# Weight parts exactly 2048 bytes apart, moving operands placed 64 bytes lower modulo 512, and a bias table of 16 copies

## The chip, the cores and the metric

The kernel runs on one core of one Trainium2 chip. The metric is the device time of one execution in microseconds, as the median of several runs.

## What is computed

Two layers of a decoder trunk on 256 tokens of width 2048, in float32. Layer 0 mixes with compressed, selected and sliding-window attention (8 heads) beside a retention group; layer 1 mixes with a gated delta rule (32 heads). Each layer then has cross-attention into 256 memory tokens and a SwiGLU FFN of hidden width 5632. Cut to its frame:

```python
def reference(x, mem, rel_bias, ...):
    h = x
    for layer in range(DEPTH):
        hn = rms_norm(h, ln_mix[layer])
        if layer % 2 == 0:
            mix = nsa_retention_mixer(hn, hyb_w_in[e], hyb_w_out[e], ..., rel_bias)
        else:
            mix = gated_deltanet_mixer(hn, gdn_w_in[o], ..., gdn_w_out[o])
        h = h + mix
        h = h + memory_cross_attention(rms_norm(h, ln_mem[layer]), mem, ...)
        h = h + swiglu_ffn(rms_norm(h, ln_ffn[layer]), ffn_w_in[layer], ffn_w_out[layer])
    return h
```

Inside the attention a bias per head depends on the distance of query and key alone: `rel_bias[rel_bucket(dist)]`.

## The kernel before

Nearly all work is projections, and all weights are read from HBM once. A projection (`Proj`, L228 by way of `passes`) takes blocks of 512 weight columns. SyncE loads 512 KB at a time (`load_weight`, L212: two rows of 128 inputs by 512 columns) into `wp`, four buffers. ScalarE rounds each row to float32r as `w_hi` (L205), VectorE forms the remainder `w_lo` (L206), both into the pool `wh`, four buffers of each. The activations are split likewise into a high and a low part (`x_hi`, `x_lo`; `hh`, `hl` in the FFN; `moh`, `mol` and others). TensorE then forms three products of each row: high by high, low by high, high by low.

In most projections the weights stand in the array (128 x 128) and the activations move, 256 columns a matmul, 12 matmuls for a weight row of 512 columns. Where the result is wanted by tokens (kind "t" in `Proj.row`), the activations stand and the weights move, 512 columns a matmul, six for a row. Moving data and the next matmul's weights both come from SBUF.

Where a tile lies in SBUF follows from its pool: pools and the tiles in them stand one behind the other in the order in which they are opened and asked for. `wh` gives every buffer the size of the largest tile asked of it. That is the row of 536 columns (2144 bytes) of the one projection in `nsa_keys` that has 256 + 280 columns, so its buffers stand 2144 bytes apart, and the pools behind it follow from there.

The bias table: `rel_bias_tiles` forms, for 8 heads, a row `f` of 400 biases by distance, on 8 partitions. It writes this row 128 times for each head to the HBM tensor `d_bias` (L735), and reads it back (L738) with a step of 399, so that each of 128 partitions of `tbias` gets its row shifted by one. Both DMAs are issued by POOL. The next ones on POOL's queue are `d_v` and `d_k` of the cross-attention (L541, L540), written when their tiles are done.

Small tasks (heads, norms, the solver) are generators that `tick` advances between the projection's matmuls; the final order on each engine is the scheduler's, from its own estimate. `invert` runs a triangular inverse on VectorE beside projections of layer 1.

Of the kernel before, what the change touches and what calls it, by code (L numbers as in the profile page):

```python
# [10 lines left out]
F32 = mybir.dt.float32  # L11
F32R = mybir.dt.float32r
# [6 lines left out]
P = 128  # L19
# [59 lines left out]
def trunk(ctx: ExitStack, tc: tile.TileContext, a: dict, out: bass.AP, phases=ALL):  # L79
    nc = tc.nc  # L80
    V, S, G, PE = nc.vector, nc.scalar, nc.gpsimd, nc.tensor
# [3 lines left out]
    wp = ctx.enter_context(tc.tile_pool(name="wp", bufs=4))  # L85
    wh = ctx.enter_context(tc.tile_pool(name="wh", bufs=4))
    sp = ctx.enter_context(tc.tile_pool(name="sp", bufs=2))
    dp = ctx.enter_context(tc.tile_pool(name="dp", bufs=1, space=DRAM))
    psj = ctx.enter_context(tc.tile_pool(name="psj", bufs=4, space=PSUM))
    psg = ctx.enter_context(tc.tile_pool(name="psg", bufs=4, space=PSUM))  # L90

    def pool(name, bufs=1, side=None):
        return tc.tile_pool(name=name, bufs=bufs, side=side, reuse_waits="tile")
# [3 lines left out]


    tasks = []
    state = {"now": 0, "banks": 4}  # L100

    class Task:
        def __init__(self, gen):
# [25 lines left out]
    def take(n):  # L129

        while state["banks"] < n:
            yield 1
        state["banks"] -= n

    def give(n):
        state["banks"] += n

    def bank(name="g"):
        return psg.tile([P, 512], F32, tag="g", name=name)
# [55 lines left out]


    def split_weight(w, g=None):
        h = wh.tile(list(w.shape), F32R, tag="wh", name="w_hi")
        l = wh.tile(list(w.shape), F32R, tag="wl", name="w_lo")
        if g is not None:  # L200

            state["hi"] = S.activation(h, w, AF.Copy, scale=g)
            V.scalar_tensor_tensor(l, w, g, h.bitcast(F32), ALU.mult, ALU.subtract)
            return h, l
        state["hi"] = S.activation(h, w, AF.Copy)  # L205
        V.tensor_sub(l, w, h.bitcast(F32))  # L206
        return h, l
# [81 lines left out]
    def proj(W, c0, segs, x, KT=KD, g=None):  # L289
        return Proj(W, c0, segs, x, KT, g).run()  # L290
# [39 lines left out]
    def split_x(tp):  # L330
        xh = tp.tile([P, KD, T], F32R, name="x_hi")
        xl = tp.tile([P, KD, T], F32R, name="x_lo")
        return xh, xl

    def fill_x(x, which, layer, rb=None):
        for k in range(KD):
            fill_k(x, which, layer, k, rb)
        return parts(x)
# [206 lines left out]
    def cross_attention(l, side):  # L545
        with pool("xax", side=side) as xx, pool("xas") as xs, pool("xa", 2) as xp:
            xb = split_x(xx)
            x = fill_x(xb, 1, l)
            kt = xs.tile([P, 4, T], F32, name="kt")
            vt = xs.tile([P, 2, 512], F32, name="vt")  # L550
            S.dma_start(kt, kv[l][0])
            S.dma_start(vt, kv[l][1])
            ec = xs.tile([P, 2], F32, name="ec")
            oh = xs.tile([P, 4, T], F32R, name="xoh")
            ol = xs.tile([P, 4, T], F32R, name="xol")

            def stat():

                yield from take(1)
                token_stat(ec)  # L560
                give(1)
                V.tensor_scalar(ec, ec, EPS, EPS * EPS, ALU.mult, ALU.add)

            def head(h, src):
                q = xp.tile([P, T], F32, tag="q", name="q")
                S.activation(q, src, AF.Copy)
                yield 1
                yield from take(2)
                sc, b2 = bank("sc"), bank("qT")
                st = xp.tile([P, 12], F32, tag="st", name="st")  # L570
                token_sumsq(q, [st[:, 6:7], st[:, 7:8]], b2)
                for t in range(2):
                    PE.matmul(sc[:, t * 256 : (t + 1) * 256], q[:, t * P : (t + 1) * P], kt[:, h, :], start=True, stop=True)
                V.scalar_tensor_tensor(st[:, 6:8], st[:, 6:8], 1.0 / P, ec, ALU.mult, ALU.add)
                rq = st[:, 8:10]
                rsqrt_(rq, st[:, 6:8], st[:, 10:12])
                s3 = sc.rearrange("p (t m) -> p t m", t=2)
                V.tensor_reduce(st[:, 0:2], s3, AX.X, ALU.max)
                V.scalar_tensor_tensor(st[:, 0:2], st[:, 0:2], -1.0, rq, ALU.mult, ALU.mult)
                p = xp.tile([P, 2, 256], F32, tag="p", name="p")  # L580
                for t in range(2):
                    S.activation(
                        p[:, t, :], s3[:, t, :], AF.Exp, scale=rq[:, t : t + 1], bias=st[:, t : t + 1],
                        accum_out=st[:, 2 + t : 3 + t],
                    )
                V.reciprocal(st[:, 4:6], st[:, 2:4])
                for t in range(2):
                    V.tensor_scalar_mul(p[:, t, :], p[:, t, :], st[:, 4 + t : 5 + t])
                yield 4
                for t in range(2):  # L590
                    for m in range(2):
                        PE.transpose(sc[:, m * 256 + t * P : m * 256 + (t + 1) * P], p[:, t, m * P : (m + 1) * P], ident)
                pT = xp.tile([P, 512], F32, tag="pT", name="pT")
                S.activation(pT, sc, AF.Copy)
                yield 1
                o = b2[:, 256:512]
                for m in range(2):
                    PE.matmul(o, vt[:, m, h * P : (h + 1) * P], pT[:, m * 256 : (m + 1) * 256], start=m == 0, stop=m == 1)
                S.activation(oh[:, h], o, AF.Copy)
                V.tensor_sub(ol[:, h], o, oh.bitcast(F32)[:, h])  # L600
                give(2)

            hs = []
            for h in range(4):
                pq = proj(a["xa_wq"][l], h * P, [("f", P)], x)[0]
                if h == 0:
                    finish([spawn(stat())])
                hs.append(spawn(head(h, pq[0][:, 0, :])))

            def xo(k):  # L610
                finish(hs[k : k + 1])
                return oh[:, k, :], ol[:, k, :]

            residual(a["xa_wo"][l], xo, 4, early=3, free=True)
# [75 lines left out]
    def mix0(xb, close):  # L690
        W = a["hyb_w_in"][0]
        done = {}
        with pool("m0o") as op:
            oh = op.tile([P, 16, T], F32R, name="moh")
            ol = op.tile([P, 16, T], F32R, name="mol")
            cm = op.tile([P, 512 + 4 * 384 + 1], F32, name="cmix")
            S.dma_start(cm, a["c_mix"])
            with pool("ns") as np_:
                x = parts(xb)
                ck = pool("cmpk", side="right")  # L700
                nsa, cmp = nsa_keys(W, x, np_, ck.__enter__(), cm)
                with pool("nt", 2) as nt:
                    for blk in range(2):
                        pq = proj(W, blk * 512, [("f", 512)], x)[0]
                        for i in range(4):
                            h = blk * 4 + i
                            q = nt.tile([P, T], F32, tag="q", name="q", bufs=8)
                            S.activation(q, pq[i // 2][:, i % 2, :], AF.Copy)
                            done[h] = spawn(nsa(nt, h, q, oh, ol))
                    finish(cmp)  # L710
                    ck.__exit__(None, None, None)
                    with pool("rt", 2) as rt_:
                        retention(W, x, rt_, oh, ol, cm, done)

                        def mo(k):
                            finish([done[k]])
                            return oh[:, k, :], ol[:, k, :]

                        residual(a["hyb_w_out"][0], mo, 16, early=12)
                        drain()  # L720
            close()

    def rel_bias_tiles(tp, rp):

        rbt = rp.tile([33, 8], F32, name="rbt")
        G.memset(rbt[32:33, :], 1.0)
        S.dma_start(rbt[:32, :], a["rel_bias"])
        ohs = rp.tile([33, 400], F32, name="ohs")
        S.dma_start(ohs, a["c_onehot"])
        b = bank()  # L730
        PE.matmul(b[:8, :400], rbt, ohs, start=True, stop=True)
        f = rp.tile([8, 400], F32, name="frev")
        V.tensor_copy(f, b[:8, :400])
        d = dp.tile([8, P, 400], F32, name="d_bias")
        G.dma_start(d, f[:, None, :].to_broadcast([8, P, 400]))  # L735
        tb = tp.tile([P, 8, 272], F32, name="tbias")

        G.dma_start(tb, bass.AP(d.tensor, d.offset + 127, [[399, P], [P * 400, 8], [1, 272]]))  # L738
        return tb

    def nsa_keys(W, x, np_, ck, cm):
# [774 lines left out]
```

## Time and profile before

| | |
|---|---|
| median of 3 runs | 3120.89 us (3120.4 to 3122.44) |
| the profiled execution | 3124.7 us, of it the span 3122.9 us |
| TensorE busy | 3042.0 us, 22,981 matmuls |
| VectorE busy | 2040.2 us |
| ScalarE busy | 1702.7 us |
| read from HBM | 549 MB, 181 GB/s over the span with what is written |

Matmuls are pipelined: the duration of one reaches beyond the start of the next. How fast TensorE goes is therefore read from starts, either of neighbouring rows in the timeline or as the length of a stretch over the number of matmuls in it. The trace leaves buffer numbers out of names; which buffer a weight row uses follows from the built program's order.

### The profile page before, as it was taken

How to read it: one execution, taken by the hardware profiler on the slowest of the kernel's cores; microseconds unless marked ns; L12 is line 12 of the kernel's file. 1: busy time of each engine (PE TensorE's matmuls, PEld its weight loads, DVE VectorE, ACT ScalarE, POOL GpSimd, SP SyncE). 2: the span in 40 equal slices, each digit the busy share in tenths (PEclk: the TensorE clock that was granted, in tenths of full speed). 3: DMA queues.
4: the chain of work that ended last, by engine and by line, in shares of the span. 5: the costliest groups of instructions: out<-in, count | busy, mean ns of one | idle time of the engine just before them, and what ended most of it. 6: DMA issues, size and time to landing. Idle time of an engine off the chain costs nothing.

```text
span 3122.9 us, 59624 instructions
## 1 busy us (share of the span) xinstructions
PE 3042.0 (97%) x22981; PEld 2912.5 (93%) x22981; DVE 2040.2 (65%) x3879; ACT 1702.7 (55%) x3316; POOL 108.8 (3%) x146
## 2 busy tenths in 40 slices
PE   9799999999999999999989978999999999999999
PEld 8699899999999999999978978999999999999887
DVE  6576776776555555557679967887567555565554
ACT  6456555664444454446655646776556444445444
POOL 0000000000000000000110100222000000000000
PEclk9899999999999999999999989999999999999999
DMA  7576545656666665556687557654555666666554
GB/s 236 145 237 197 156 130 178 189 167 187 185 184 188 184 188 184 188 186 181 178 226 220 173 151 200 175 156 126 187 182 176 184 183 187 184 186 183 196 197 164
DMA packets 340026, 569.99 MB, mean 183 GB/s; under 512 B 43844, under 2 KB 83828, under 8 KB 339612
## 3 DMA queue, kind: packets, MB, share of 16 engines
q1 hardware_dynamic: 333376, 550.79, 59.1%
q0 software_dynamic: 3056, 9.26, 1.2%
q10 hardware_dynamic: 3308, 6.14, 0.6%
q8 instruction: 180, 2.95, 0.4%
q14 instruction: 106, 0.87, 0.1%
HBM read 549.16 MB, written 15.37 MB: 181 GB/s over the span
## 4 chain that ended last, share of the span: by engine, by line
PE 94%; DMA 2%; DVE 2%; SPq 1%; ACT 0%; issue 0%; POOL 0%; DVEq 0%; ACTq 0%; POOLq 0%
PE pj L228 87%; DMA w<-in_hyb_w_in 1%; SPq L1344 1%; PE cmp L228 1%; DMA w<-in_gdn_w_in 1%; PE slv L1426 0%; PE slv L1437 0%; DVE w_lo L206 0%; PE slv L1440 0%; DVE xT L415 0%; DMA d_T<-AB 0%; DVE x_lo L348 0%; DMA mraw<-in_mem 0%; PE slv L1434 0%; PE slv L1420 0%
## 5 line engine op out<-in xcount | busy, mean ns | idle before, releaser
L206 DVE TENSOR_TENSOR w_lo<-w,w_hi 128x512 fp32r<-128x512 f32 x1938 | 1334.0, 693 | 951.2 <-ACT w_hi L205 937.8
L205 ACT ACTIVATE w_hi<-w 128x512 fp32r<-128x512 f32 x1938 | 1220.8, 632 | 1238.9 <-PE pj L228 968.3
L228 PE MATMUL pj<-x_hi,w_hi 128*128 128x256 f32 (+1 forms) x4496 | 1264.3, 283 | 50.4 <-ACT w_hi L205 50.1
L228 PE MATMUL pj<-x_lo,w_hi 128*128 128x256 f32 x4496 | 1265.6, 284 | 0.0
L228 PE MATMUL pj<-x_hi,w_lo 128*128 128x256 f32 (+1 forms) x4496 | 1241.8, 283 | 0.3 <-DVE w_lo L206 0.2
L228 PEld LDWEIGHTS pj<-x_hi,w_hi 128*128 128x128 f32 (+1 forms) x4496 | 848.9, 189 | 52.4 <-ACT w_hi L205 50.7
L228 PEld LDWEIGHTS pj<-x_lo,w_hi 128*128 128x128 f32 x4496 | 850.0, 189 | 1.1 <-issue 0.2
L228 PEld LDWEIGHTS pj<-x_hi,w_lo 128*128 128x128 f32 (+1 forms) x4496 | 836.0, 189 | 2.0 <-DVE w_lo L206 1.1
L228 PE MATMUL pj<-hh,w_hi 128*128 128x256 f32 x704 | 197.1, 281 | 0.0
L228 PE MATMUL pj<-hl,w_hi 128*128 128x256 f32 x704 | 197.1, 281 | 0.0
L228 PE MATMUL pj<-o,w_hi 128*128 128x256 f32 x1024 | 192.8, 287 | 3.0 <-ACT o L996 1.8
L228 PE MATMUL pj<-hh,w_lo 128*128 128x256 f32 x704 | 195.5, 280 | 0.0
L228 PE MATMUL pj<-w_lo,x_hi 128*128 128x512 f32 (+2 forms) x448 | 173.7, 388 | 3.4 <-DVE w_lo L206 3.4
L228 PE MATMUL pj<-w_hi,x_lo 128*128 128x512 f32 (+2 forms) x448 | 171.5, 383 | 0.0
L228 PEld LDWEIGHTS pj<-o,w_hi 128*128 128x128 f32 x1024 | 160.9, 192 | 4.1 <-ACT o L996 2.3
L228 PE MATMUL pj<-w_hi,x_hi 128*128 128x512 f32 (+2 forms) x448 | 145.6, 387 | 4.6 <-ACT w_hi L205 4.6
L228 PE MATMUL pj<-o,w_lo 128*128 128x256 f32 x512 | 145.7, 288 | 0.0
L228 PE MATMUL pj<-w_hi,hl 128*128 128x512 f32 x352 | 138.8, 394 | 0.0
L228 PE MATMUL pj<-w_lo,hh 128*128 128x512 f32 x352 | 138.7, 394 | 0.0
L228 PEld LDWEIGHTS pj<-hh,w_hi 128*128 128x128 f32 x704 | 132.8, 189 | 0.0
L228 PEld LDWEIGHTS pj<-hl,w_hi 128*128 128x128 f32 x704 | 132.5, 188 | 0.0
L228 PEld LDWEIGHTS pj<-hh,w_lo 128*128 128x128 f32 x704 | 131.9, 188 | 0.0
(414 smaller groups left out, 3628.9 us busy)
## 6 DMA issues: line engine op xcount, KB each, us to landing
w<-in_ffn_w_in SPq DMA_DIRECT2D x352, 512.0 KB
w<-in_gdn_w_in SPq DMA_DIRECT2D x193, 512.0 KB
w<-in_ffn_w_out SPq DMA_DIRECT2D x176, 512.0 KB
w<-in_hyb_w_in SPq DMA_DIRECT2D x96, 512.0 KB
w<-in_gdn_w_out SPq DMA_DIRECT2D x64, 512.0 KB
w<-in_xa_wkv SPq DMA_DIRECT2D x32, 512.0 KB
w<-in_hyb_w_out SPq DMA_DIRECT2D x32, 512.0 KB
w<-in_nsa_cmp_w SPq DMA_DIRECT2D x16, 512.0 KB
```

The source lines that it names most:

```text
L205: state["hi"] = S.activation(h, w, AF.Copy)
L206: V.tensor_sub(l, w, h.bitcast(F32))
L228: PE.matmul(o, s_, m, start=start and j == 0, stop=last and j == 2, skip_group_check=True)
L1344: nc.sync.dma_start(bass.AP(dst.tensor, dst.offset, [[64 * 512, 8], [512, 64], [1, 128]]), AB[p0 : p0 + 15 : 2].rearrange("p i w j -> p i ...
```

## The change

Three things are edited.

1. Rows of more than 512 columns take their parts from a pool of their own (`wide`, two buffers of 640 columns), opened around `nsa_keys` alone. The buffers of `wh` are then 2048 bytes.
2. A tile of 448 bytes, `pad`, is put into the pool `sp`, so that the pools behind it begin at other places; in `cross_attention` the small tile `ec` is asked for after `xoh` and `xol`.
3. `d_bias` holds 16 copies of a row for each head, not 128, and is read back into `tbias` by eight DMAs of 16 partitions each.

The places of the tiles in the built programs, in bytes modulo 512 (column blocks and rows of these tiles follow in steps of 512 or 1024 bytes, so that the remainder is that of every operand):

| tile | before | after |
|---|---|---|
| w_hi, buffers 0, 1, 2, 3 | 32, 128, 224, 320 | 32, 32, 32, 32 |
| w_lo, buffers 0, 1, 2, 3 | 416, 0, 96, 192 | 32, 32, 32, 32 |
| x_hi, x_lo (mixers and FFN), o0 to o7 | 480 | 480 |
| hh, hl, moh, mol, mh, ml, o8 to o15, x_hi and x_lo of one cross-attention | 288 | 480 |
| xoh, xol | 320 | 480 |
| w_hi, w_lo of the 536-column rows | as w_hi, w_lo | 320 |

The diff:

```diff
     sp = ctx.enter_context(tc.tile_pool(name="sp", bufs=2))
+
+    sp.tile([P, 112], F32, name="pad", bufs=1)
+    state = {"now": 0, "banks": 4, "wide": None}
     dp = ctx.enter_context(tc.tile_pool(name="dp", bufs=1, space=DRAM))
...
     def split_weight(w, g=None):
-        h = wh.tile(list(w.shape), F32R, tag="wh", name="w_hi")
-        l = wh.tile(list(w.shape), F32R, tag="wl", name="w_lo")
+
+        n = int(np.prod(w.shape[1:]))
+        if n > 512:
+            h, l = (
+                state["wide"].tile([P, 1, 640], F32R, tag=t, name=m)[:, :, :n] for t, m in (("wh", "w_hi"), ("wl", "w_lo"))
+            )
+        else:
+            h = wh.tile(list(w.shape), F32R, tag="wh", name="w_hi")
+            l = wh.tile(list(w.shape), F32R, tag="wl", name="w_lo")
...
-            ec = xs.tile([P, 2], F32, name="ec")
             oh = xs.tile([P, 4, T], F32R, name="xoh")
             ol = xs.tile([P, 4, T], F32R, name="xol")
+            ec = xs.tile([P, 2], F32, name="ec")
...
-                nsa, cmp = nsa_keys(W, x, np_, ck.__enter__(), cm)
+                with pool("wide", 2) as state["wide"]:
+                    nsa, cmp = nsa_keys(W, x, np_, ck.__enter__(), cm)
...
-        d = dp.tile([8, P, 400], F32, name="d_bias")
-        G.dma_start(d, f[:, None, :].to_broadcast([8, P, 400]))
+        d = dp.tile([8, 16, 400], F32, name="d_bias")
+        G.dma_start(d, f[:, None, :].to_broadcast([8, 16, 400]))
         tb = tp.tile([P, 8, 272], F32, name="tbias")
 
-        G.dma_start(tb, bass.AP(d.tensor, d.offset + 127, [[399, P], [P * 400, 8], [1, 272]]))
+        for p0 in range(0, P, 16):
+            G.dma_start(tb[p0 : p0 + 16], bass.AP(d.tensor, d.offset + 127 - p0, [[399, 16], [16 * 400, 8], [1, 272]]))
```

On POOL's queue, where the bias table is written and read, there stands before:

```order
L735 DMA d_bias<-frev 1024x1x400
L541 DMA d_v_1406<-vt 128x1024
L540 DMA d_k_1405<-kt 128x1024
L738 DMA tbias<-d_bias 128x8x272
L749 MEMSET kcat 128x2x16
L750 MEMSET vc 128x256
```

and after (lines 10 further down in the file):

```order
L745 DMA d_bias<-frev 128x1x400
L550 DMA d_v_1407<-vt 128x1024
L549 DMA d_k_1406<-kt 128x1024
L749 DMA tbias<-d_bias 16x8x272 x8
L760 MEMSET kcat 128x2x16
L761 MEMSET vc 128x256
```

The places in the queue are the same; the write is an eighth as long, and the read is eight DMAs in a row.

On ScalarE, where the 16 rows of 536 columns are split (beside the squares `hsq` and the root `hr` of a key norm), there stands before:

```order
L205 ACTIVATE w_hi<-w 128x512 x7
L205 ACTIVATE w_hi<-w 128x536 x3
L358 ACTIVATE hsq<-pj 128x256
L205 ACTIVATE w_hi<-w 128x536
L358 ACTIVATE hsq<-pj 128x256
```

and after:

```order
L214 ACTIVATE w_hi<-w 128x512 x5
L214 ACTIVATE w_hi<-w 128x536
L214 ACTIVATE w_hi<-w 128x512
L214 ACTIVATE w_hi<-w 128x536
L214 ACTIVATE w_hi<-w 128x512
L367 ACTIVATE hsq<-pj 128x256 x2
```

The first wide splits moved ahead, between the last narrow ones of the projection before. Outside this stage and the solver stage of layer 1, where some small tasks change places with their neighbours, the order of all engines is that of before.

## Rows read from the trace of the kernel before

**Rows 1.** The page: busy time of the engines, and the chain by line.
```profile
PE 3042.0 (97%) x22981; PEld 2912.5 (93%) x22981; DVE 2040.2 (65%) x3879; ACT 1702.7 (55%) x3316; POOL 108.8 (3%) x146
...
PE pj L228 87%; DMA w<-in_hyb_w_in 1%; SPq L1344 1%; PE cmp L228 1%; DMA w<-in_gdn_w_in 1%; PE slv L1426 0%; PE slv L1437 0%; DVE w_lo L206 0%; PE slv L1440 0%; DVE xT L415 0%; DMA d_T<-AB 0%; DVE x_lo L348 0%; DMA mraw<-in_mem 0%; PE slv L1434 0%; PE slv L1420 0%
```

**Rows 2.** Groups of TensorE's matmuls by form: count | busy us, mean ns.
```profile
L228 PE MATMUL pj<-x_lo,w_hi 128*128 128x256 f32 x4480 | 1261.7, 284 | 0.0
...
L228 PE MATMUL pj<-w_lo,x_hi 128*128 128x512 f32 x384 | 155.5, 405 | 3.4 <-DVE w_lo L206 3.4
```

**Rows 3.** Busy time and counts by engine in stretches of the projections.
```profile
core 0: us, PE busy (x) PEld busy (x) DVE busy (x) ACT busy (x) POOL busy (x), PEclk, DMA share, GB/s
525.00:575.00 50.00, 50.00 (x428) 50.00 (x427) 32.45 (x60) 27.82 (x53) 0.00 (x0) 1.00 0.59 185
700.00:1150.00 450.00, 450.00 (x3795) 450.00 (x3795) 264.79 (x436) 222.19 (x358) 0.00 (x0) 1.00 0.65 186
1170.00:1400.00 230.00, 230.00 (x1953) 230.00 (x1952) 124.08 (x198) 109.98 (x186) 0.00 (x0) 1.00 0.57 187
1690.00:1840.00 150.00, 150.00 (x1162) 145.17 (x1162) 140.35 (x226) 89.67 (x191) 13.88 (x11) 1.00 0.64 186
...
2420.00:2840.00 420.00, 420.00 (x3546) 420.00 (x3546) 245.71 (x404) 205.19 (x331) 0.00 (x0) 1.00 0.65 185
2900.00:3100.00 200.00, 200.00 (x865) 162.03 (x864) 102.90 (x151) 91.21 (x144) 0.00 (x0) 1.00 0.59 197
```

**Rows 4.** Timeline of TensorE, first FFN (start us, us, what): beginnings of rows.
```profile
1101.05 0.28 PE L228 MATMUL pj<-x_hi,w_hi 128*128 128x256 f32 x1
...
1102.47 0.29 PE L228 MATMUL pj<-x_hi,w_hi 128*128 128x256 f32 x1
...
1103.18 0.28 PE L228 MATMUL pj<-x_hi,w_hi 128*128 128x256 f32 x1
...
1103.87 0.28 PE L228 MATMUL pj<-x_hi,w_hi 128*128 128x256 f32 x1
...
1105.30 0.28 PE L228 MATMUL pj<-x_hi,w_hi 128*128 128x256 f32 x1
...
1106.75 0.28 PE L228 MATMUL pj<-x_hi,w_hi 128*128 128x256 f32 x1
```

**Rows 5.** Timeline of TensorE in the first FFN's second half, on buffer 2.
```profile
1257.41 0.28 PE L228 MATMUL pj<-hh,w_hi 128*128 128x256 f32 x1
...
1258.43 0.28 PE L228 MATMUL pj<-hh,w_hi 128*128 128x256 f32 x1
```

**Rows 6.** Timeline of ScalarE in the rows of 536 columns.
```profile
199.10 0.65 ACT L205 ACTIVATE w_hi<-w 128x536 fp32r<-128x536 f32 x1 [0.83 <-PE pj L228]
200.56 0.65 ACT L205 ACTIVATE w_hi<-w 128x536 fp32r<-128x536 f32 x1 [0.81 <-PE pj L228]
```

**Rows 7.** Waits in 120 to 165 us: total us, times, longest.
```profile
ACT w_hi L205 <- DMA w<-in_hyb_w_in: 28.1, 2, 20.9
...
PE pj L228 <- ACT w_hi L205: 20.4, 2, 16.9
```

**Rows 8.** The tensor d_bias: the read's issue on POOL, and both landings.
```profile
L738 POOL DMA_DIRECT2D tbias<-d_bias x1: 931/931/931, 163.2 to 163.2; - x1
...
DMA to landing us min/median/max: 10.6/23.8/37.0
```

**Rows 9.** Stretches as in rows 3, around the early stall.
```profile
113.00:150.00 37.00, 16.30 (x107) 14.74 (x105) 9.70 (x21) 8.01 (x19) 0.55 (x1) 0.74 0.65 119
150.00:155.00 5.00, 5.00 (x25) 4.95 (x25) 4.51 (x10) 2.92 (x8) 0.00 (x0) 0.53 0.57 174
```

**Rows 10.** Timeline of TensorE in layer 1, a row on buffer 0.
```profile
1814.65 0.28 PE L228 MATMUL pj<-x_hi,w_hi 128*128 128x256 f32 x1
...
1815.90 0.28 PE L228 MATMUL pj<-x_hi,w_lo 128*128 128x256 f32 x1
```

**Rows 11.** Timeline of ScalarE at the same time.
```profile
1814.74 0.64 ACT L205 ACTIVATE w_hi<-w 128x512 fp32r<-128x512 f32 x1 [0.41 <-PE pj L228]
```

More of the change, by code (lines that the diff above doesn't have):

```diff
@@ L99, in trunk @@
     tasks = []
-    state = {"now": 0, "banks": 4}
     class Task:
```

## The prediction

> **What bounds the kernel now.** I began with the page. TensorE is busy 97% of the span, and 87% of the chain of work that ended last are the projection matmuls of L228 [rows 1]; VectorE follows with 65%. So the time is the number of these matmuls times the step from one start to the next, plus some stretches in which TensorE waits. The mean durations in the grouped view (284 and 405 ns) overlap and are no step; I use the counts alone. Added up over its groups (the two largest forms stand in [rows 2]), L228 has 18,912 matmuls with 256 columns and 2,400 with 512.
>
> The step comes from stretches in which nothing else runs on TensorE, as length over count [rows 3]. 450/3795 is 118.6 ns and 420/3546 is 118.4 ns (the first halves of the two FFNs); 230/1953 is 117.8, 50/428 is 116.8; with 512 columns 200/865 is 231.2. [...]
>
> Then I went to single matmuls, beside the table of buffer places further up. In the FFN a weight row is 12 matmuls of one form, and the rows go over four pairs of buffers; only the place of w_hi and w_lo differs. In [rows 4] a row begins on buffer 3 at 1101.05, on 0 at 1102.47, on 2 at 1103.87, on 1 at 1105.30 and on 3 again at 1106.75: they take 1.42, 1.40, 1.43 and 1.45 us. Inside the row on buffer 0 two regimes stand side by side: 1102.47 to 1103.18 is six steps of 118 ns, 1103.18 to 1103.87 six of 115 with the last one's change of buffer in it. How low the second regime goes is seen in the FFN's second half, where the moving operand lies at 288 and not at 480, on buffer 2: from 1257.41 to 1258.43 nine steps in 1.02 us [rows 5], **113.3 ns**. I call this the floor.
>
> What the two fast cases share is a distance. Moving at 480 with weights at 32 and 416 (buffer 0): +64 and -64. Moving at 288 with weights at 224 and 96 (buffer 2): -64 and -192. All are odd multiples of 64 bytes. The slow pairs lie at 160/32, 256/128 and -160/224 from 480, and at -256/128, -160/224 and 32/-96 from 288: odd multiples of 32, or multiples of 128. I read this as two streams out of SBUF, weights and moving, which hinder each other unless they are half a 128-byte line apart, and a few matmuls in which the phase settles after each change of distance.
>
> **The change, part by part.**
>
> *One distance everywhere.* After the change each pair lies at 32 and each moving operand at 480: +64 throughout, save 192 matmuls of the wide rows. No row changes the distance, so all should stay at the floor. In the stretches of [rows 3] the gain is 3795 x 5.3 + 3546 x 5.1 + 1953 x 4.5 + 428 x 3.5 ns = 48 us for 9,722 matmuls. The other 9,190 stand in mixed stages; they get the 4.5 ns of the middle: 41 us (3.5 to 5.3 gives 32 to 49). Together 89 us.
>
> With 512 columns the roles are exchanged (weights move, activations stand), at the same 64. Twice the floor is 226.6 ns; against 231.2 that is up to 2,400 x 4.6 = 11 us. No stretch shows this step held, so I take 8, with 0 and 11 as ends.
>
> Three things take some back. Where other matmuls break in, the phase must settle again, as at the head of the row on buffer 0 (6 x 5 ns). The page counts 22,981 matmuls, about 1,570 outside L228; in blocks of some four that is 390 restarts, at half that price 6 us. In 1690 to 1840, VectorE is busy 140 of 150 us [rows 3] with the triangular inverse beside the splits: of the 1162 x 4.5 ns = 5 us there I give up half. In the solver stage the scheduler's order shifts a little and TensorE waits on chains of other engines: 2 us.
>
> *The wide rows.* Sixteen weight rows of 536 columns get a pool of two buffers, not a share of four. A split there takes ScalarE 0.65 us, one per 1.46 us, after 0.8 us of waiting [rows 6]. The matmuls of one row cover the split of the next, so this can cost nothing; if w_lo came late by one split each time, 16 x 0.65 = 10 us. I take 2, nearer the end that the 0.8 us of slack speak for.
>
> *The bias table.* TensorE's one early stall lies in 113 to 150 us: it waits 20.4 us for w_hi, and behind that ScalarE 28.1 us for weight loads of in_hyb_w_in [rows 7]. Meanwhile the 1600 KB write of d_bias, from 8 partitions, is under way, 37.0 us to landing [rows 8], with d_v behind it on POOL's queue, and the core moves 119 GB/s [rows 9] against 186 in the FFN. [...] The change writes an eighth, at the same rate 4.6 us, done before TensorE runs out of rows. I take 21 us, between 10 (one load still late) and 23. The reading back to tbias becomes eight transfers behind d_k on POOL, at most 0.93 us of issue each [rows 8]: the memsets behind them start up to 6.5 us later, and their readers, the heads, come only after the compressed keys. The bytes are the same; the read of before landed in 10.6 us and no wait of TensorE falls there. Cost 0, at worst 5 us of held-up loads.
>
> **Sum.** 89 + 8 - 6 - 2.5 - 2 - 2 + 21 = 105.5 us. The profiled execution took 3124.7 us (span 3122.9 and 1.8 around it): 3019. It lies 3.8 us above the median of the runs; from the median, 3120.9, I get **3015 us**.
>
> **The rivals.** (1) *Places do not matter to TensorE.* The uneven steps would come from something else that goes with the buffers, such as ScalarE's turn, and only the bias edit remains: 3121 - 21 = 3100. Against it stand steps of 113, 118 and 121 ns at one clock and one form. Chance 0.05. [...]
>
> (2) *Half the gain.* The slow half of the row on buffer 0 lies under ScalarE's split of a later row. After the change these splits write at 32 modulo 512, the place from which TensorE reads weights; before, the place written and the place read always differ. If a split held the step at 118, for 0.63 of 1.40 us, that is 0.45 x 4.7 ns x 18,912 = 40 us: 3055. Against it: on buffer 0 from 1814.65 to 1815.90 eleven steps take 1.25 us, 113.6 each [rows 10], with a split running from 1814.74 on for 0.64 us [rows 11]. Chance 0.09.
>
> (3) *Slower.* +64 for both parts at once is not in the trace. If with one distance for all the phase settled in a slow step, say buffer 1's 121 ns, the loss is 18,912 x 2.7 ns = 51 us, less 21: 3151. It decides from a mean step of about 119.4 ns on (18,912 x 1.1 ns = 21 us). Against it: on buffer 0 two matmuls in a row read w_hi at +64, and they come to the floor. Chance 0.05.
>
> (4) *The stall stays*, because the loads are late for a reason other than d_bias: 3036. Chance 0.03.
>
> **How the numbers follow.** The forecast has 0.78. Its own ends (mixed stages -9 or +8, 512 columns -8 or +3, wide rows -8 or +2, bias -11 or +2) do not all fall together; half of each sum gives 3007 to 3033, all of it 3000 to 3051. The range goes beyond rival 2 and stops short of 1 and 3: **2994 to 3062**. Within 0.2% (6 us, about what a measurement of this kernel can tell from no change) ends only a weak form of 1 or 3. Faster 0.93, same 0.02, slower 0.05.
>
> **What would show it.** The 450 us from 700 should hold about 3,970 matmuls, not 3,795, and weight rows should take 1.36 us on every pair. TensorE should have no wait over 3 us in 113 to 150, with the clock at 1.00, and d_bias should land in under 8 us. Steps of 118 under each split would be rival 2; unchanged steps rival 1; steps over 120 rival 3. The forecast also fails if the splits or the weight loads, which must come 4% faster, become what TensorE waits for: the FFN would need 195 GB/s, and the last stage already runs at 197 [rows 3].

## The result, and the profile after

The changed kernel takes **3033.39 us** (median; 3029.89 to 3038.68), the kernel before 3120.99 beside it: a ratio of 0.972, 95% interval 0.9703 to 0.9737. The forecast was 3015 in a range of 2994 to 3062. The profiled execution took 3029.9 us, 94.8 less than that of before; the sum of the prediction had 105.5. Line numbers are up to 11 higher than before: L228 is L237, L205 and L206 are L214 and L215, L735 and L738 are L745 and L749.

The first view is the page's busy times, which answer to the head of [rows 1].

```profile
PE 2962.2 (98%) x22981; PEld 2839.1 (94%) x22981; DVE 2034.9 (67%) x3879; ACT 1698.0 (56%) x3316; POOL 111.9 (4%) x153
```

TensorE still sets the time, and its 22,981 matmuls now take 80 us less. The same stages as in [rows 3] (they begin earlier now), and the place of the early stall:

```profile
525.00:575.00 50.00, 50.00 (x427) 50.00 (x426) 35.19 (x70) 29.48 (x59) 0.00 (x0) 1.00 0.60 185
680.00:1120.00 440.00, 440.00 (x3885) 440.00 (x3884) 270.96 (x447) 226.78 (x366) 0.00 (x0) 1.00 0.67 195
2350.00:2550.00 200.00, 200.00 (x1767) 200.00 (x1766) 120.76 (x199) 101.64 (x164) 0.00 (x0) 1.00 0.67 193
2550.00:2750.00 200.00, 200.00 (x1704) 200.00 (x1703) 119.75 (x199) 99.03 (x160) 0.00 (x0) 1.00 0.65 187
2800.00:3000.00 200.00, 200.00 (x876) 164.08 (x875) 103.91 (x153) 92.28 (x146) 0.00 (x0) 1.00 0.61 199
113.00:150.00 37.00, 35.70 (x312) 35.50 (x310) 30.16 (x54) 19.95 (x37) 6.20 (x14) 1.00 0.86 234
1640.00:1780.00 140.00, 140.00 (x1183) 138.38 (x1182) 133.59 (x224) 88.16 (x188) 13.37 (x10) 1.00 0.63 182
```

- The first FFN is where the prediction wanted it: 440/3885 is 113.3 ns, with 118.6 before.
- The second FFN is split. Up to 2550 the step is 200/1767, 113.2 ns; from there on 200/1704, **117.4 ns**, with the same code, the same buffers and distances and the same clock.
- 525 to 575 (`hyb_w_out`, the output projection of layer 0's mixer) gained nothing: 427 matmuls where [rows 3] had 428.
- The 512-column step is 200/876, 228.3 ns, after 231.2.
- In 113 to 150 TensorE is idle for 1.3 us and not 20.7, and the clock is 1.00.

On the early stall, the waits in 110 to 165 us (total us, times, longest) and the tensor d_bias:

```profile
ACT w_hi L214 <- DMA w<-in_hyb_w_in: 8.8, 3, 5.6
...
PE pj L237 <- ACT w_hi L214: 2.2, 1, 2.2
```
```profile
L749 POOL DMA_DIRECT2D tbias<-d_bias x8: 530/531/561, 134.6 to 139.0; - x8
...
DMA to landing us min/median/max: 5.9/9.0/13.9
```

The 20.4 us of [rows 7] are 2.2, and the write of d_bias, 37.0 us in [rows 8], lands in 5.9 (the least of the nine; the reads alone have 7.0 as their least).

What remained to explain was the 117-ns stretch. It begins between two matmuls. TensorE's timeline of the changed kernel (start us, us, what) shows two interruptions of one kind, by the transposes of L672:

```profile
2516.14 0.49 PE L672 MATMUL g<-ident,xT 128*128 128x128 f32 x3
...
2516.59 0.28 PE L237 MATMUL pj<-x_hi,w_hi 128*128 128x256 f32 x1
...
2520.11 0.28 PE L237 MATMUL pj<-x_hi,w_hi 128*128 128x256 f32 x1
```
```profile
2560.01 0.27 PE L672 MATMUL g<-ident,xT 128*128 128x128 f32 x1
...
2560.24 0.28 PE L237 MATMUL pj<-x_hi,w_hi 128*128 128x256 f32 x1
...
2564.01 0.28 PE L237 MATMUL pj<-x_lo,w_hi 128*128 128x256 f32 x1
```

Behind the first, 31 steps take 3.52 us, 113.5 ns; behind the second, 32 steps take 3.77 us, **117.8 ns**, and so it stays for 1,866 matmuls. The first is three transposes, the second one.

Then all starts of the trace were counted: a *stretch* is ten or more steps between 256-column projection matmuls with no other matmul and no pause between them, and it counts as long if its last six steps average 116.5 ns or more. The changed kernel has 77 short stretches, which end at 113.3 to 114.2 ns, and 47 long ones, all but one of which end at 117.7 or 117.8. The long ones have 4,221 matmuls (the 1,866 among them, and 748 in `hyb_w_out`), and apart from the first matmuls there is hardly any change within a stretch. The theory: **at one distance for all, there are two steady steps; each interruption picks one, and it holds until the next.** Rivals: those stages have another cause of their own (splits, loads, operands); or the distance does not matter, only that it is equal for all rows.

### The profile page after: what moved, and what is told of

Its sections match the earlier page's. It is cut to its first block, busy times and chain, and to the rows that moved or that the text cites. A ratio compares the mean times of both kernels' runs of the same rounds, so it can differ in the third digit from the quotient of the medians.

```text
span 3028.1 us, 59625 instructions
## 1 busy us (share of the span) xinstructions
PE 2962.2 (98%) x22981; PEld 2839.1 (94%) x22981; DVE 2034.9 (67%) x3879; ACT 1698.0 (56%) x3316; POOL 111.9 (4%) x153
## 4 chain that ended last, share of the span: by engine, by line
PE 95%; DVE 2%; DMA 2%; SPq 1%; ACT 1%; issue 0%; POOL 0%; DVEq 0%; ACTq 0%; POOLq 0%
PE pj L237 87%; SPq L1355 1%; PE cmp L237 1%; DMA w<-in_hyb_w_in 1%; DVE w_lo L215 1%; PE slv L1451 0%; PE slv L1448 0%; PE slv L1437 0%; DMA w<-in_gdn_w_in 0%; DVE xT L424 0%; DMA d_T<-AB 0%; DVE x_lo L357 0%; PE slv L1445 0%; DMA mraw<-in_mem 0%; PE kk L1065 0%
## 5 line engine op out<-in xcount | busy, mean ns | idle before, releaser
L215 DVE TENSOR_TENSOR w_lo<-w,w_hi 128x512 fp32r<-128x512 f32 x1938 | 1329.6, 692 | 862.7 <-ACT w_hi L214 847.6
L214 ACT ACTIVATE w_hi<-w 128x512 fp32r<-128x512 f32 x1938 | 1217.1, 631 | 1141.0 <-DVE w_lo L215 589.8
L237 PE MATMUL pj<-x_hi,w_hi 128*128 128x256 f32 (+1 forms) x4496 | 1247.0, 280 | 36.5 <-ACT w_hi L214 36.1
L237 PE MATMUL pj<-x_lo,w_hi 128*128 128x256 f32 x4496 | 1246.1, 279 | 0.0
L237 PE MATMUL pj<-x_hi,w_lo 128*128 128x256 f32 (+1 forms) x4496 | 1226.0, 280 | 1.2 <-DVE w_lo L215 1.2
L237 PEld LDWEIGHTS pj<-x_hi,w_hi 128*128 128x128 f32 (+1 forms) x4496 | 848.2, 189 | 39.2 <-ACT w_hi L214 37.5
L237 PEld LDWEIGHTS pj<-x_lo,w_hi 128*128 128x128 f32 x4496 | 845.2, 188 | 1.1 <-issue 0.2
L237 PEld LDWEIGHTS pj<-x_hi,w_lo 128*128 128x128 f32 (+1 forms) x4496 | 831.4, 188 | 3.0 <-DVE w_lo L215 2.2
L237 PE MATMUL pj<-hl,w_hi 128*128 128x256 f32 x704 | 193.7, 276 | 0.0
L237 PE MATMUL pj<-hh,w_hi 128*128 128x256 f32 x704 | 193.6, 276 | 0.0
L237 PE MATMUL pj<-hh,w_lo 128*128 128x256 f32 x704 | 192.4, 276 | 0.0
L237 PE MATMUL pj<-o,w_hi 128*128 128x256 f32 x1024 | 184.8, 283 | 2.0 <-ACT o L1007 1.6
L237 PE MATMUL pj<-w_lo,x_hi 128*128 128x512 f32 (+2 forms) x448 | 172.1, 385 | 3.5 <-DVE w_lo L215 3.5
L237 PE MATMUL pj<-w_hi,x_lo 128*128 128x512 f32 (+2 forms) x448 | 169.5, 379 | 0.0
L237 PEld LDWEIGHTS pj<-o,w_hi 128*128 128x128 f32 x1024 | 157.3, 191 | 2.8 <-ACT o L1007 2.1
L237 PE MATMUL pj<-w_hi,x_hi 128*128 128x512 f32 (+2 forms) x448 | 142.6, 384 | 4.4 <-ACT w_hi L214 4.4
L237 PE MATMUL pj<-o,w_lo 128*128 128x256 f32 x512 | 142.3, 282 | 0.0
L237 PE MATMUL pj<-w_hi,hl 128*128 128x512 f32 x352 | 138.3, 393 | 0.0
L237 PE MATMUL pj<-w_lo,hh 128*128 128x512 f32 x352 | 137.7, 391 | 0.0
L237 PEld LDWEIGHTS pj<-hl,w_hi 128*128 128x128 f32 x704 | 132.2, 188 | 0.0
L237 PEld LDWEIGHTS pj<-hh,w_hi 128*128 128x128 f32 x704 | 132.2, 188 | 0.0
L237 PEld LDWEIGHTS pj<-hh,w_lo 128*128 128x128 f32 x704 | 131.3, 188 | 0.0
```

The costliest lines, as they stand in the source:

```text
L237: PE.matmul(o, s_, m, start=start and j == 0, stop=last and j == 2, skip_group_check=True)
```

## The experiments

All are made from the changed kernel unless said otherwise. Weights are moved against a moving operand that stays at 480, so distance and place were not told apart. Counted from the starts, as above (behind the number of long stretches that of their matmuls; in the kernel before the distances change from row to row; in zero 102 of the 124 stretches end within 0.4 of 120.0 ns, the others at 118.0 to 120.7; the 512-column step is the mean over all stages that have it):

| kernel | w_hi, w_lo from the moving operand | stretches: short, long (matmuls) | 512-column step, ns | median us |
|---|---|---|---|---|
| before | many | 21, 103 (12,863) | 231.8 | 3120.99 |
| after | +64, +64 | 77, 47 (4,221) | 229.1 | 3033.39 |
| after_again | +64, +64 | 75, 47 (4,270) | 229.1 | 3033.88 |
| lo_minus64 | +64, -64 | 115, 10 (516) | 231.1 | 3025.69 |
| hi_minus64 | -64, +64 | 81, 46 (1,282) | 231.8 | 3031.59 (one run) |
| all_minus64 | -64, -64 | 11, 113 (16,705) | 233.3 | 3096.36 |
| all_plus192 | +192, +192 | 12, 113 (15,628) | 233.3 | 3091.63 (one run) |
| zero | 0, 0 | 0, 124 (17,401) | 227.1 | 3121.75 |

The kernel before took 3123.0 to 3124.4 us beside all but the first two rows.

**The two edits apart.** The placement with d_bias left at 128 copies:

> The placement edits alone (d_bias stays at 128 copies). If the two edits are independent, as the sum of the prediction has it: the after kernel plus the 21 us of the early stall, 3054 us, with TensorE's waits of some 20 us in 100 to 160 us back. If the early stall was already shortened by other means (the projections there run faster or slower and meet the loads elsewhere): 3033 to 3045 us.

The old places with the bias table's edit:

> The bias table's edit alone, at the old places. Independent edits: 3121 - 21 = 3100 us, steps as before (428 matmuls in the 50 us of hyb_w_out, 3,795 in 450 us of the FFN). If the stall stays because loads are late for another reason (rival 4): 3118 to 3122 us.

Measured: 3054.34 (ratio 0.9781, 0.9766 to 0.9796) and 3100.99 (0.9926, 0.9911 to 0.9941), as the sum had them. The stretch 113 to 150 us, of the first and of the second:

```profile
113.00:150.00 37.00, 16.96 (x110) 15.54 (x109) 9.89 (x23) 8.64 (x19) 0.55 (x1) 0.71 0.63 118
```
```profile
113.00:150.00 37.00, 36.68 (x301) 35.96 (x300) 32.78 (x60) 21.91 (x40) 6.21 (x14) 1.00 0.83 219
...
700.00:1150.00 450.00, 450.00 (x3796) 450.00 (x3796) 264.78 (x437) 222.10 (x358) 0.00 (x0) 1.00 0.63 185
```

The stall comes and goes with the copies alone, and with the copies alone the step stays as it was (3,796 matmuls in the first FFN's 450 us, 3,795 before). The one edit is worth 70.0 us, the other 23.4; both together were 89.6 beside the same kind of run (after_again, 3123.51 to 3033.88), 4 us less than the two added up, which is within the intervals.

**Distance 0 for all.**

```diff
+    wg.tile([P, 112], F32, name="gap")      # a pool ahead of wh
     wh = ctx.enter_context(tc.tile_pool(name="wh", bufs=4))
-    sp.tile([P, 112], F32, name="pad", bufs=1)
```

> As the after kernel, but all weight parts at 480 modulo 512, so that weights and moving operands lie at a distance of 0, again equal for all rows. Theory that the distance matters and a multiple of 128 is slow: FFN steps of 118 to 120 ns (before, the buffer at -256/+128 ran at 119.1), no stretch at 113.3, total 3095 to 3115 us. Rival, that equal distance in all rows is the whole gain, whatever the distance is: stretches at 113.3 as in the after kernel, total 3028 to 3040 us.

Measured: 3121.75, a ratio of 0.9993 (0.9983 to 1.0002), although the bias edit is in it. The first FFN, and the 512-column stage:

```profile
700.00:1100.00 400.00, 400.00 (x3335) 400.00 (x3335) 230.47 (x378) 193.10 (x313) 0.00 (x0) 1.00 0.64 183
...
2920.00:3090.00 170.00, 170.00 (x752) 140.77 (x751) 89.99 (x132) 79.01 (x125) 0.00 (x0) 1.00 0.61 203
```

400/3335 is **119.9 ns**. It is 120.0 under ScalarE's splits alone (1,309 steps of this window), under VectorE's alone (1,520) and under both (501), so it does not hang on which of them is writing. Equal distance is therefore not the gain. But 170/752 is **226.1 ns**: for 512 columns the worst place of all is the best. That was not expected.

**Signs.** For w_lo at -64, a gap of 96 elements stands between the pools of w_hi and w_lo and the pad shrinks to 16; for all at -64, the gap stands ahead of both.

> As the after kernel, but w_lo at 416 and not 32 modulo 512: w_hi at +64, w_lo at -64 from the moving operand, which before was the case on buffer 0 alone. In the after kernel each uninterrupted run of matmuls takes one of two steps, 113.3 or 117.8 ns, and keeps it to its end (some 3,900 matmuls in runs at 117.8). Theory: the interruption picks the step, and two equal distances hold either; where they change sign within a row the slow one does not hold (before, 4 of 226 rows on buffer 0 stayed slow). Then all long stretches come to 113.3 after some 6 steps of 118, hyb_w_out's 50 us hold 441 matmuls and not 427, the first half of the second FFN 3,705 in 420 us and not 3,648, total 3010 to 3020 us. Rival, that the slow stretches come from something else in those stages (splits, loads, the operands' columns): hyb_w_out stays at 425 to 428 per 50 us, total 3028 to 3040 us.

> As the after kernel, but w_hi and w_lo both at 416 modulo 512, 64 bytes below the moving operand and not above it. If the distance counts modulo 128 only, +64 and -64 are the same: long stretches at 113.3 or 117.8 as in the after kernel, some of them locked at 117.8, total 3025 to 3045 us. If the sign matters (the slow step exists only on one side): all long stretches at 113.3, total 3008 to 3020 us, or all at one slower step, total over 3050 us.

> As the after kernel, but w_hi at 416 and w_lo at 32: w_hi at -64 and w_lo at +64, the signs of the fast kernel exchanged. Both at -64 gave 117.8 ns nearly everywhere, both at +64 either 113.3 or 117.8. Theory that a change of sign within the row, whichever way, does not let the slow step hold: long stretches at 113.3, total 3018 to 3032 us. Rival, that each matmul's step follows its own sign (two of three matmuls read w_hi): means of 116 to 118 ns in the FFNs, total 3060 to 3100 us.

> As the after kernel, but both weight parts at 160 modulo 512, 192 bytes from the moving operand and not 64. The prediction's rule, that every odd multiple of 64 bytes is good: long stretches at 113.3 or locked at 117.8 ns, total 3015 to 3097 us, and some stretches at 113.3. If only plus or minus 64 is good: no stretch at 113.3, steps of 118 ns and more, total over 3097 us.

lo_minus64, in hyb_w_out, in the second FFN, and with 512 columns:

```profile
525.00:575.00 50.00, 50.00 (x444) 50.00 (x443) 36.66 (x72) 30.67 (x62) 0.00 (x0) 1.00 0.62 195
...
2600.00:2720.00 120.00, 120.00 (x1061) 120.00 (x1060) 75.04 (x125) 61.84 (x100) 0.00 (x0) 1.00 0.67 194
2800.00:3000.00 200.00, 200.00 (x867) 162.63 (x866) 102.97 (x150) 91.34 (x145) 0.00 (x0) 1.00 0.59 198
```

Both stages that were at the long step now run at 113 ns (50/444 and 120/1061). Of 1,295 weight rows with no break in them, 1,289 end with six steps below 115.5 ns on average (after: 1,005 of 1,297), and a start at 117 to 122 ns mostly falls back within some 15 matmuls. The total, 3025.69 (0.9685, 0.9669 to 0.9702), missed the forecast of 3010 to 3020. With 256 columns 14.5 us were gained (23.4 us above the floor became 8.9), but the 512-column step rose by 2 ns, 2,400 x 2 = 4.8 us, which the forecast had left out; the difference, 9.7, stands beside 3033.88 - 3025.69 = 8.2 us.

all_minus64 and all_plus192, first FFN:

```profile
700.00:1100.00 400.00, 400.00 (x3399) 400.00 (x3398) 237.24 (x391) 197.74 (x320) 0.00 (x0) 1.00 0.59 187
```
```profile
700.00:1100.00 400.00, 400.00 (x3399) 400.00 (x3398) 237.45 (x391) 197.68 (x320) 0.00 (x0) 1.00 0.65 186
```

Both 117.7 ns; both know the short step too (in all_plus192 one stretch of 1,214 matmuls keeps it), but it is rarely picked. So the distance does not count modulo 128: at -64 113 of 124 stretches are long, at +64 47 of 124. The two kernels have the same step with 512 columns, and of the 122 stretches that can be set side by side only three end at different steps; one of them, the stretch of some 1,210, makes most of the gap between 16,705 and 15,628 matmuls. As -64 and +192 are the same modulo 256, the runs are in keeping with a distance that counts modulo 256, with +64 and +192 as two unlike places that share the two steps and differ in which is picked. With the signs exchanged (hi_minus64), the first FFN holds 3,532 matmuls in 400 us, 113.3 ns, but 46 stretches, most of them of a few dozen matmuls, end at the long step.

**Interruptions put in.** Ten times in the first half of the first FFN, where the changed kernel has none:

```diff
+    for n in (1, 3, 1, 2, 1, 3, 1, 2, 1, 3):
+        ...
+        for f in range(n):
+            PE.transpose(p[:, f * P : (f + 1) * P], xT[:, f, :P], ident)
+        give(1)
+        yield 33
```

> The after kernel with ten interruptions of 1, 3, 1, 2, 1, 3, 1, 2, 1, 3 small transposes (idle work, 128 x 128, results not read) put between the projection matmuls of the first half of the first FFN, some 397 matmuls apart. In the after kernel that half has none, and 6,142 matmuls in a row run at 113.3 ns. Theory that an interruption picks one of two steps, which then holds until the next: between two interruptions all steps, after the first few, are either 113.3 or 117.8 ns, they change at interruptions alone, and some of the ten lead to 117.8 (in the rest of the after kernel 46 of 124 uninterrupted stretches did). Each stretch of 397 at 117.8 costs 1.8 us; total 3033 to 3048 us with the interruptions' own 2 to 4 us. Rival, that the slow stretches belong to certain stages and have another cause there: all eleven stretches stay at 113.3 and only 2 to 4 us are added.

> The same ten interruptions in the kernel with w_lo at 416 and w_hi at 32. Theory that a change of sign within each row does not let the slow step hold: all eleven stretches are back at 113.3 within some 15 matmuls after an interruption. Rival, that this kernel's long stretches were fast by the luck of their interruptions: some of the eleven run at 116 ns or more to their end.

Four of the stretches between them, behind 3, 1, 3 and 1 transposes, of the changed kernel with the ten:

```profile
710.00:750.00 40.00, 40.00 (x355) 40.00 (x355) 25.23 (x42) 20.41 (x33) 0.00 (x0) 1.00 0.63 197
755.00:795.00 40.00, 40.00 (x342) 40.00 (x341) 24.43 (x41) 19.79 (x32) 0.00 (x0) 1.00 0.59 189
895.00:935.00 40.00, 40.00 (x356) 40.00 (x355) 24.73 (x42) 20.86 (x34) 0.00 (x0) 1.00 0.60 191
940.00:980.00 40.00, 40.00 (x342) 40.00 (x342) 24.01 (x40) 20.22 (x33) 0.00 (x0) 1.00 0.59 187
```

and the second and fourth of the same stretches with w_lo at -64:

```profile
755.00:795.00 40.00, 40.00 (x355) 40.00 (x354) 24.67 (x41) 20.71 (x34) 0.00 (x0) 1.00 0.61 191
...
940.00:980.00 40.00, 40.00 (x355) 40.00 (x354) 22.96 (x37) 20.50 (x34) 0.00 (x0) 1.00 0.62 197
```

Six of the ten led to 117.8 ns and held it for all 394 steps to the next one; four led to 113.3. Three transposes led to the short step each time (3 of 3 here, 5 of 5 in the second FFN), two to the long one (2 of 2), one mostly (4 of 5 here, 1 of 1 there). With signs +64 and -64 all ten came back to 113.3. Against the same kernels without the ten, the stage grew by 12.7 us in the first and by 2.5 in the second; the difference, 10.2, is close to 6 x 394 x 4.45 ns = 10.5. The totals, one run each, were 3051.97 and 3035.68. The first is 4 us above its forecast; its solver stage took 7 us more than that of the kernel without the ten, for a reason that was not followed up.

**The same kernel again.**

> The after kernel once more. If what an interruption picks is set by the program (the number of matmuls that break in, their places), the same stretches as in the first profile run at 117.8 ns (748 matmuls of hyb_w_out, 1,866 of the second FFN's first half), and the median is 3033 us within 4. If it is chance from run to run, other stretches are slow in this profile, and the times spread by some 10 us.

Measured: 3033.88 (3026.63 to 3035.71; ratio 0.9708, 0.9695 to 0.9721). Of 122 stretches that begin at the same place in both profiled executions, 115 end at the same step, the 748 and the 1,866 among them. Seven do not: they have 10 to 150 matmuls, and the one of 150, in the second FFN, is long in the first execution and short in the second. So the program sets most of what an interruption picks, but not all of it. The times spread by 9 us, about what was expected of chance. One execution of each run was profiled, so whether more stretches turn over in the others is not shown.

**512 columns apart.** In lo64_hh0, hh and hl of the second FFN stand 64 bytes further up; in by_kind, w_hi and w_lo share a buffer and take their places by the kind of projection.

> The kernel with w_lo at 416 and w_hi at 32, and in the second FFN hh and hl 64 bytes further up, at 32, where they serve only the 512-column matmuls of the second half (1,056 of them): there the distances are 0 and 384, multiples of 128. With all parts at a distance of 0, 512-column steps took 227.0 ns, with +64 some 229, with +64 and -64 some 231. Theory that for 512 columns a multiple of 128 is the good distance: 1,056 x 3.5 to 4 ns = 4 us less than without the shift, some 3020 to 3023 us, 200 us of the last stage holding 881 matmuls. Rival, that only the exact distance 0 or equal parts do it: 3024 to 3028 us, no change.

> The two parts of a weight row in one buffer, placed by the kind of projection: where activations move in 256 columns, w_hi at +64 and w_lo at -64 from them (long stretches at 113.3 ns in the kernel with w_lo at 416); where the weights move in 512 columns, both parts at a distance of 0 (227.0 ns with all parts there, against a mean of 231.2 with +64 and -64 and 229.1 with +64 alone). If the two kinds are independent: 2,400 x 4 ns = 9.6 us less than the 3025.7 us with w_lo at 416 alone, 3012 to 3019 us, and the last stage holds 881 matmuls in 200 us. If one buffer for both parts holds up ScalarE's splits until the last matmul of a row (a wait that the two separate pools do not have): 3020 to 3035 us, with TensorE waiting for w_hi.

The last stage of lo64_hh0 and of by_kind, and the solver stage of lo_minus64 and of by_kind:

```profile
2800.00:3000.00 200.00, 200.00 (x872) 163.18 (x871) 103.93 (x151) 91.54 (x146) 0.00 (x0) 1.00 0.58 198
```
```profile
2800.00:3000.00 200.00, 200.00 (x884) 165.58 (x884) 105.25 (x154) 92.97 (x148) 0.00 (x0) 1.00 0.60 201
```
```profile
1980.00:2100.00 120.00, 118.13 (x1012) 116.50 (x1010) 97.35 (x246) 87.80 (x251) 27.58 (x38) 1.00 0.57 157
```
```profile
1980.00:2100.00 120.00, 113.69 (x949) 110.42 (x947) 92.56 (x234) 86.02 (x240) 23.30 (x35) 0.99 0.52 150
```

With the exact distance 0 for both parts the step is 226.2 ns (884), with 0 and 384 bytes 229.4 (872), and 231 before that shift: a multiple of 128 will not do. lo64_hh0 took 3020.67 (0.9672, 0.9656 to 0.9688). That is a total which the theory had foretold, but not for its reason: of the 5.8 us between the profiled executions of lo_minus64 and lo64_hh0, 4.6 were there before the first matmul that reads the shifted tiles, for a cause that was not followed up. by_kind took 3023.04 (0.9679, 0.9665 to 0.9692). At the first of the solver's matmuls it was 8.8 us ahead of lo_minus64, at the last 0.9: in the stretch shown TensorE is idle for 6.3 us and not 1.9. It waits there for solver tiles and for `o`, and never for weights, so the expected wait for a shared buffer is not what cost the time. The order of that stage came out differently with one buffer for both parts; that this is the reason was not tried apart. All three beat the kernel before and the changed kernel as first measured (interval from 0.9703), lo_minus64 only just (to 0.9702); its interval overlaps that of after_again (from 0.9695). Among themselves the three overlap.

## Why the prediction was nearly right, and where it was wrong

*The bound and the floor* held: TensorE's step decides, and 113.3 ns is reached in 13,164 matmuls, where [rows 4, 5] had it for parts of rows. The count for the first FFN comes out as foretold (3,885 in 440 us are 3,973 in 450).

*"No row changes the distance, so all should stay at the floor"* is the step that failed. Added up over the steps above 113.3 ns, the 256-column matmuls lay 90.8 us above the floor before and 23.4 after: 67.4 us gained, where the sum had 89 - 6 - 2.5 = 80.5. Of the 23.4, **18.3 us are the 47 stretches at 117.8 ns**. The rest, 5.1 us, is the settling after interruptions, for which 6 was put in. VectorE's stage (1640 to 1780 above) has no wait of TensorE (busy for 140.00 us of 140) and gave nothing back.

What misled was buffer 0. Its rows came to 113 within six steps, and the prediction read that as "odd multiples of 64 are good", against rival 3 too. But buffer 0 was +64 *and* -64, and buffer 2 in [rows 5] -64 and -192: modulo 256 both are 64 and 192, two distances in each row. Just this did not let the long step stand in lo_minus64, which has the pair of buffer 0: 115 of its 125 stretches end at the short step, 77 of 124 in the changed kernel. The changed kernel made them equal and so took away what had brought the rows down. Rival 3 was the right doubt; it came true for a quarter of the matmuls and at 117.8, not 121.

That the change took +64 and no other odd multiple of 64 was luck. By the prediction's rule every one of them would do, but -64 and +192 gave 3096.36 and 3091.63, only 5 and 9 us below the bias edit alone (3100.99).

*512 columns:* (231.8 - 229.1) x 2,400 = 6.5 us, put in with 8. The size was right, the reason (the same 64 bytes are good) wrong.

*The bias table:* 20 us in the two windows of [rows 9], 23.4 alone, put in with 21. No run shows the 23 us of its upper end as such: [rows 9] show 20.7 us of idle time and, in the 5.00 us behind it, 25 matmuls at a granted clock of 0.53, where 42 steps of 118.6 ns have room (some 2 us, an estimate). After the change the same windows have 1.3 and 1.2 us of idle time, at a clock of 1.00. *Wide rows:* from 180 to 260 us TensorE has one wait, of 0.6 us; put in were 2.

*Given back, and not foreseen:* in layer 1 SyncE issues the sixteen stores of d_T (L1344, now L1355), and TensorE waits for weights meanwhile. The stores on SyncE and TensorE's wait, before and after:

```profile
1842.37 32.90 SPq L1344 DMA_DIRECT2D d_T<-AB  x16
...
PE pj L228 <- ACT w_hi L205: 29.7, 1, 29.7
```
```profile
1771.68 35.57 SPq L1355 DMA_DIRECT2D d_T<-AB  x16
...
PE pj L237 <- ACT w_hi L214: 33.3, 1, 33.3
```

Of the 3.6 us, 2.7 are the stores, which take SyncE longer. It is not that TensorE is faster now: it runs dry some 11.6 us behind the first store in both, and zero, whose steps are the slowest, waits 33.3 us too. Every run with the new places waits 32.8 to 35.0 us, and bias_only 29.7 as before. Why the places make the stores slower is open.

Together 67.4 + 6.5 + 20 - 3.6 = 90 of the 94.8 us between the profiles; the rest lies in mixed stages. The profiled execution of the changed kernel is the fastest of its four, and that of before lies 3.7 us above its median, so the medians show 87.6.

*Rival 1* is out: zero and after differ in nothing but places and by 88 us, with steps of 119.9 and 113.3 ns in the first FFN at the same granted clock of 1.00. *Rival 2* is out: from 680 to 1120 ScalarE starts its splits as before, and the step is 113.3 throughout. *Rival 4* is out by bias_only.

**Still open:** why a distance makes a step long (that two streams hinder each other was the author's reading; no run shows what waits for what), why the long step is steady, why 256 and 512 columns want opposite places, and what in an interruption picks the step (the number of transposes also changes how long it lasts). Absolute places were not varied apart from distances, and that 256 is the period rests on two pairs of places.

## What to carry to other kernels

Where one engine sets the time, measure its step from starts in stretches with nothing between, and look at single steps: a mean of 115 can be two levels, here 113.3 and 117.8. A good stretch may be good because of what varies in it, so copy all of it when you generalise, or try the uniform case first. And after a change, look for a stretch that did not move; here two of them, with 748 and 1,866 matmuls at 4.45 ns too much, held 11.6 us, most of the 13.1 by which the step's gain fell short.

## What the runs showed of the hardware

- A 256-column projection step had discrete levels that went with the places of weights and moving operand in SBUF: 113.3, 117.8 and 120.0 ns at a granted clock of 1.00. At one distance (+64 bytes) two levels were both steady, 117.8 ns over 1,866 and 113.3 over 6,142 matmuls in a row.
- Which level came went with what broke in: behind three 128-column transposes 113.3 in 8 of 8, behind two 117.8 in 2 of 2, behind one 117.8 in 5 of 6. It is not fixed: 7 of 122 stretches ended at the other level when the same kernel ran again.
- With w_hi at +64 and w_lo at -64 it came back to 113.3 behind all ten interruptions put in, and in 115 of 125 stretches.
- With 512 columns the order is turned round: 226.2 ns at a distance of 0, 229 at +64, 231 at +64 and -64, 233.3 at -64.
